# A fp32 two-layer trunk on one NeuronCore: P1 ahead of E0 in the recurrence layer's program

## The chip, the cores and the metric

The kernel runs on one core of a Trainium2 chip. The metric is the device time of one launch in microseconds (us); less is better. Times are medians of several runs, and one run was also taken with the hardware profiler.

## The reference

The input x is (1, 512, 1024) in fp32. Layer 0 mixes the tokens with an RWKV-7 recurrence, layer 1 with a spatial gating unit; a SwiGLU feed-forward network follows each, and RMS norms stand before and behind every part. The change lies in layer 0:

```python
xs = x[None] + xx[None] * mix[:, None, None, :]
r, k, v = jnp.einsum('cbtd,cde->cbte', xs[:3], w_rkv)
decay = jnp.exp(-jnp.exp(w_log)); a = jax.nn.sigmoid(a0 + (xa @ a1) @ a2)
kk = heads(k * k_k); kk = kk / max(norm(kk), 1e-12)
k = k * (1.0 + (a - 1.0) * k_a)
S_t = S_{t-1} diag(w_t) + (S_{t-1} a_t) b_t^T + v_t k_t^T      # 16 heads of 64, 512 steps
y_t = S_t r_t
```

with a_t = -kk and b_t = kk times a. The kernel computes the recurrence in chunks of 64 tokens: cumulative decays, products of pairs within a chunk, the inverse of a triangular matrix per chunk and head, and then a scan over the 8 chunks.

## The kernel before, in words

The 16 heads are worked in four batches b of 256 features, each two feature tiles q of 128. `rwkv()` (L669) walks through the words of the string `PLAN` (L35). The word's letter names a stage and its digit the batch:

```python
for n in PLAN:
    f, b = n[0], int(n[1])
    if f == "P":
        if xr is None:
            xr = mixed_split(0, "ssssssss")
        kr[b] = kr_proj(b)
    elif f == "E":
        ops[b] = early(b, *kr[b])
```

- **P**, `kr_proj` (L807): the projections to k and r. Four units (k for q 0 and 1, then r), each 24 matmuls of 128x512 (tile `proj`), since every fp32 product is made of three: whi with both halves of the activations (`xsp`) and wlo with the upper half. `weight()` (L184) loads a unit's weights by SP's queue into `wraw`, ScalarE casts them to `whi` (L181) and VectorE subtracts to make `wlo` (L182). There are two buffers each of wraw, whi and wlo, so a unit's cast waits for the matmuls of the unit two before it. ScalarE copies the result out of PSUM (L813).
- **E**, `early(b)` (L893): two small matmuls for decay and a; on ScalarE tanh, exponentials (L923, L925) and, for the norm of kk, L936, L940, L941, L942, with table loads between different functions; on VectorE the steps L916, L919 (a scan over the tokens), L926, L932, L945 to L951, L954, L961, L962; on TensorE the norm's sums (`ssp`, L938) and the bonus sums (`bps`, L957). SP's queue stores four results to DRAM, two to `sa` (L964) and two to `sb` (L967). Batches 0 and 2 share one set of buffers for the tiles `tw` and `ta`, batches 1 and 3 another (`tws`).
- **V**, `v_proj` (L851): the value projection, two units of 48 matmuls of 128x256 (`v`) per word, eight units in all, called u0 to u7 here; weights by `weight()` as above, results copied out (`vev`, L867) and stored (`Vd`, L868).
- **F**, `front(b)` (L977): loads `ST` from sb (L982) and `MV` from sa (L988, 16 loads), then makes the products of pairs: eight `lm` (L1004) and four `bkt` (L1018) in two PSUM banks that they share. ScalarE empties an lm with three copies (L1007, L1010, L1012) and a bkt with four (L1022, L1023), and GpSimd cuts triangles out of the copies (L972).
- **B**, `back(b)` (L1026): the inverse. VectorE transposes `LA` to `LX` (L1035), goes through 15 dependent steps of a product (`tm`, L1049) and a subtraction (`Dm`, L1051), and transposes twice (`hn` L1054, `Dt` L1055). TensorE then multiplies blocks up: `mvt` (L1062), `Qp` (L1071), `Np` (L1080), `Tp` (L1083), `Q2p` (L1094), `T2p` (L1103), `mp` (L1112), `gh` (L1119), into `bdT`.
- **X** prepares the value projection's activations, **S**, `scan` (L1124), goes through the chunks, and **N**, `finish`, does the group norm and the gate.

The words give the program's order only. Which instruction comes where on each engine is set by a list scheduler (`schedule_with_timeline_sim=True`, L1428), which takes the program's order as priority and interleaves what its own model holds ready. Each engine then works its row of instructions off in that order, and so does SP's queue of DMAs.

Of the kernel before, what the change touches and what calls it, by code (L numbers as in the profile page):

```python
# [31 lines left out]
BANKS_F1 = dict(tr=(1, 2), gu=(4, 0, 7, 6), R=(4, 0), Q=(3, 5), Z=(7, 6), h0=(1, 2, 0, 5), h1=(4, 3, 7, 6))  # L32
SLOTS = 17
E2 = 7
PLAN = "P0 E0 P1 E1 P2 E2 P3 E3 X0 F0 B0 F1 V0 V1 V2 V3 B1 S0 F2 S1 F3 N0 B2 N1 B3 S2 N2 S3 N3".split()  # L35
XV = "xxxessss"
XSLOTS = 13
LAG = 2
# [94 lines left out]
class Trunk:  # L133
# [535 lines left out]
    def rwkv(self, x0):  # L669
# [3 lines left out]
        with ExitStack() as ctx:  # L673
# [574 lines left out]
            xr, kr, ops, Y = None, {}, {}, {}  # L1248
            for n in PLAN:
                f, b = n[0], int(n[1])  # L1250
# [181 lines left out]
```

## Time and profile before

| | us |
|---|---|
| median of 3 runs | 1315.66 (1313.27 to 1319.33) |
| profiled run | 1315.28 |
| its span, first to last instruction | 1313.6 |
| outside the span | 1.7 |
| TensorE busy | 1257.4 |
| mean granted clock of TensorE | 0.984 of full speed |

A row of a timeline gives the start and length in us, the engine, the line, the operation, output<-inputs, how many instructions were joined, and in brackets the idle time before the row with what ended it. Of the span, 81 to 163 us hold the key and receptance projections, 163 to 227 the value projection with front(0) and parts of back(0) and front(1) between its matmuls, and the recurrence layer goes on up to some 480 us; the rest are the two feed-forward networks and the gating unit.

### The profile page before, as it was taken

Reading aid. Unit: us, or ns where it says so; the run is one execution under the profiler, and the core shown is the slowest. Engines: PE = TensorE matmul, PEld = TensorE weight load, DVE = VectorE, ACT = ScalarE, POOL = GpSimd, SP = SyncE. Lnnn points to the kernel's source line nnn. Section 1 sums busy time; section 2 is a strip of 40 time slices with the busy share of each in tenths; the row PEclk is TensorE's granted clock in tenths of the full one; section 3 lists DMA queues with packets and bytes.
Section 4 is the critical chain, followed back from the end, with each engine's and each line's share of the span. In section 5 each row is a group of like instructions: output and inputs, shape, how many; then the busy total and the mean of one; then the engine's idle time right before and its main releaser. Section 6 shows DMA issues by size and latency. Waiting matters only on the chain.

```text
span 1313.6 us, 24404 instructions
## 1 busy us (share of the span) xinstructions
PE 1257.4 (96%) x9644; PEld 1091.1 (83%) x9644; DVE 988.1 (75%) x1613; ACT 739.4 (56%) x1303; POOL 151.6 (12%) x300
## 2 busy tenths in 40 slices
PE   5999999989899899999999999999989999999998
PEld 3667799978787698999997878878888999998876
DVE  7976766477866687868779977476679877789985
ACT  7986785686444463445546556543454454556553
POOL 0000284566000002100000000020002000000000
PEclk9999999999979999999999999999989999999999
DMA  5137594322243225244344314343430433444322
GB/s 163 34 95 175 146 224 156 88 72 65 75 127 112 75 80 160 68 126 125 92 154 136 122 49 128 94 135 94 144 97 1 129 98 105 120 125 149 113 65 81
DMA packets 219379, 144.29 MB, mean 110 GB/s; under 512 B 67920, under 2 KB 193408, under 8 KB 219264
## 3 DMA queue, kind: packets, MB, share of 16 engines
q1 hardware_dynamic: 217968, 138.01, 36.4%
q0 software_dynamic: 1296, 4.72, 1.1%
q8 instruction: 76, 1.25, 0.4%
q14 instruction: 39, 0.32, 0.1%
HBM read 128.54 MB, written 14.16 MB: 109 GB/s over the span
## 4 chain that ended last, share of the span: by engine, by line
PE 68%; DVE 7%; ACT 2%; issue 1%; DMA 1%; POOL 0%; DVEq 0%; ACTq 0%
PE acc L206 25%; PE Q L206 10%; PE gu L206 9%; PE R L206 7%; PE Z L206 7%; PE u L206 3%; DVE wlo L182 1%; PE gh L1119 1%; PE mp L1112 1%; PE Yp L1161 1%; PE lm L1004 1%; DVE wsum L405 1%; DVE x L336 1%; PE s L1366 1%; PE ptr L281 0%
## 5 line engine op out<-in xcount | busy, mean ns | idle before, releaser
L182 DVE TENSOR_TENSOR wlo<-wraw,whi 128x1024 fp32r<-128x1024 f32 x83 | 103.1, 1244 | 66.5 <-ACT whi L181 57.7
L206 PE MATMUL Q<-bc,whi 128*128 128x256 f32 x816 | 147.3, 281 | 2.2 <-ACT hn L449 2.2
L206 PE MATMUL acc<-whi,ablk 128*128 128x512 f32 x448 | 141.6, 395 | 2.7 <-DVE acc L623 2.7
L181 ACT CAST whi<-wraw 128x1024 fp32r<-128x1024 f32 x83 | 86.9, 1050 | 101.5 <-PE acc L206 29.2
L206 PEld LDWEIGHTS Q<-bc,whi 128*128 128x128 f32 x816 | 125.5, 189 | 2.8 <-ACT hn L449 2.6
L181 ACT CAST whi<-wsum 128x1024 fp32r<-128x1024 f32 x68 | 71.1, 1051 | 85.0 <-PE Q L206 24.3
L206 PE MATMUL gu<-hT,whi 128*128 128x256 f32 (+1 forms) x448 | 112.0, 342 | 3.3 <-ACT hT L62 1.7
L206 PE MATMUL Q<-bc,wlo 128*128 128x256 f32 x408 | 114.6, 281 | 0.0
L206 PEld LDWEIGHTS acc<-whi,ablk 128*128 128x128 f32 x448 | 84.2, 188 | 23.3 <-ACT hn L621 1.8
L206 PE MATMUL Z<-bc,whi 128*128 128x256 f32 x544 | 99.8, 281 | 0.0
L206 PE MATMUL R<-bc,whi 128*128 128x256 f32 x544 | 98.7, 281 | 0.0
L182 DVE TENSOR_TENSOR wlo<-wsum,whi 128x1024 fp32r<-128x1024 f32 x68 | 82.2, 1221 | 21.5 <-ACT whi L181 20.4
L181 ACT CAST whi<-wq 128x1024 fp32r<-128x1024 f32 x51 | 53.5, 1050 | 72.3 <-PE R L206 22.9
L206 PEld LDWEIGHTS gu<-hT,whi 128*128 128x128 f32 x448 | 78.8, 197 | 13.7 <-ACT hT L62 2.4
L206 PE MATMUL acc<-wlo,ablk 128*128 128x512 f32 x224 | 88.5, 395 | 1.5 <-DVE wlo L182 1.5
L182 DVE TENSOR_TENSOR wlo<-wq,whi 128x1024 fp32r<-128x1024 f32 x51 | 65.3, 1284 | 27.6 <-ACT whi L181 27.4
L206 PEld LDWEIGHTS Z<-bc,whi 128*128 128x128 f32 x544 | 84.1, 189 | 0.0
L206 PEld LDWEIGHTS R<-bc,whi 128*128 128x128 f32 x544 | 83.8, 188 | 0.2
L206 PE MATMUL proj<-xsp,whi 128*128 128x512 f32 x256 | 82.4, 401 | 1.3 <-ACT r L813 1.3
L206 PEld LDWEIGHTS Q<-bc,wlo 128*128 128x128 f32 x408 | 77.2, 189 | 0.0
L206 PE MATMUL Z<-bc,wlo 128*128 128x256 f32 x272 | 76.3, 282 | 0.9 <-DVE wlo L182 0.9
L206 PE MATMUL R<-bc,wlo 128*128 128x256 f32 x272 | 76.6, 282 | 0.0
(377 smaller groups left out, 3191.7 us busy)
## 6 DMA issues: line engine op xcount, KB each, us to landing
wc<-in_ffn_w_down_dram SPq DMA_DIRECT2D x38, 512.0 KB, 3.9
wq<-in_ffn_w_gate_dram SPq DMA_DIRECT2D x68, 256.0 KB
wq<-in_ffn_w_up_dram SPq DMA_DIRECT2D x68, 256.0 KB, 4.7
wraw<-in_rwkv_w_rkv_dram SPq DMA_DIRECT2D x24, 512.0 KB, 5.3
wraw<-in_sgu_w_in_dram SPq DMA_DIRECT2D x16, 512.0 KB, 4.3
wraw<-in_ffn_w_gate_dram SPq DMA_DIRECT2D x10, 512.0 KB
wraw<-in_ffn_w_up_dram SPq DMA_DIRECT2D x10, 512.0 KB, 3.9
x<-in_x_dram SPq DMA_DIRECT2D x8, 512.0 KB, 3.6
```

The lines of the kernel that those rows point to most:

```text
L181: self.nc.scalar.copy(hi, src)
L182: self.nc.vector.tensor_tensor(lo, src, hi.bitcast(F32), op=ALU.subtract)
L206: self.nc.tensor.matmul(out, l, r, start=start, stop=stop, skip_group_check=resumed)
L336: v.scalar_tensor_tensor(xts[tt][:, c], f, y[:, 0:1], xts[tt][:, c], op0=ALU.mult, op1=ALU.add)
L405: v.tensor_tensor(s, x, y, op=ALU.add)
L1004: mm(lm[:, cc * P:(cc + 1) * P], st[:, cc].rearrange("p n t -> p (n t)"), mv[:, cc, :, hd, :], start=True, stop=True)
L1112: mm(mp[:, cc * P:(cc + 1) * P], bdT[:, q * NC + 4 * hh + cc].rearrange("p h t -> p (h t)"), mt[:, cc, :], start=True, stop=True)
L1119: mm(gh[:, cc * P:(cc + 1) * P], mt[rows, cc, :], bx[rows, 0:2, cc, :], start=True, stop=True)
L1161: mm(yp[yr, yc], MV[hh, q][:, cc, 1, hd, :], su[:, q, hd, :], start=True, stop=True)
L1366: mm(acc[:, tt * P:(tt + 1) * P], vt[tt][:, m * P:(m + 1) * P], wsT[:, m, :], start=True, stop=True)
```

## The change

One line differs. The projections of batch 1 come ahead of the early stage of batch 0 in the program; every function is the same.

```diff
-PLAN = "P0 E0 P1 E1 P2 E2 P3 E3 X0 F0 B0 F1 V0 V1 V2 V3 B1 S0 F2 S1 F3 N0 B2 N1 B3 S2 N2 S3 N3".split()
+PLAN = "P0 P1 E0 E1 P2 E2 P3 E3 X0 F0 B0 F1 V0 V1 V2 V3 B1 S0 F2 S1 F3 N0 B2 N1 B3 S2 N2 S3 N3".split()
```

The number of instructions on each engine stays the same. What moves is the scheduler's interleaving. First VectorE in the first two projections, where the wlo belong to P1, L945 to L950 and the first pc, Pp and k to early(0), and L916 and L919 with cum to early(1):

```order
-L182 TENSOR_TENSOR wlo<-wraw,whi 128x1024
-L926 COPY pc<-Pp 128x16
-L182 TENSOR_TENSOR wlo<-wraw,whi 128x1024
+L182 TENSOR_TENSOR wlo<-wraw,whi 128x1024 x2
 L945 SCALAR_TENSOR_TENSOR k<-k,nkk,tw 128x512 x2
 L916 TENSOR_SCALAR tws<-tws 128x1024
+L919 SCALAR_TENSOR_TENSOR cum<-rmask,tws 128x512 x2
+L182 TENSOR_TENSOR wlo<-wraw,whi 128x1024 x3
+L926 COPY pc<-Pp 128x16
 L949 TENSOR_TENSOR tw<-k,Pp 128x1024
-L919 SCALAR_TENSOR_TENSOR cum<-rmask,tws 128x512 x2
+L926 COPY pc<-Pp 128x16
```

early(0)'s L949, from which the rest of that stage hangs, stands three wlo later, and early(1)'s scan stands ahead of it. On TensorE, this is where front(0)'s last lm and bkt stand among the value projection's matmuls now, from the 186th of 384 on:

```order
L1004 MATMUL lm<-MV,ST 128x128 x4
L206 MATMUL v<-whi,xsp 128x256
L206 MATMUL v<-wlo,xsp 128x256
L206 MATMUL v<-whi,xsp 128x256 x2
L206 MATMUL v<-wlo,xsp 128x256
L206 MATMUL v<-whi,xsp 128x256
L1004 MATMUL lm<-MV,ST 128x128 x4
L1018 MATMUL bkt<-ident,ST 128x128 x4
L1004 MATMUL lm<-MV,ST 128x128 x4
L206 MATMUL v<-whi,xsp 128x256 x2
L1004 MATMUL lm<-MV,ST 128x128 x4
```

In before, the last bkt of front(0) and the first mvt of back(0) stand so, with all lm of front(0) at least ten value matmuls earlier:

```order
L1004 MATMUL lm<-MV,ST 128x128 x4
L206 MATMUL v<-wlo,xsp 128x256
L206 MATMUL v<-whi,xsp 128x256 x2
L206 MATMUL v<-wlo,xsp 128x256
L206 MATMUL v<-whi,xsp 128x256 x2
L206 MATMUL v<-wlo,xsp 128x256
L206 MATMUL v<-whi,xsp 128x256 x2
L206 MATMUL v<-wlo,xsp 128x256
L1018 MATMUL bkt<-ident,ST 128x128 x4
```

front(0)'s lm lay between the 67th and the 178th value matmul and lie between the 130th and the 194th now; the first lm of front(1) moved from the 262nd to the 310th, the first mvt from the 192nd to the 227th, and Qp from the 313th to the 330th. Last, VectorE in back(0)'s chain of 15 steps (tm and Dm), where the wlo are those of u6 and u7 of the value projection. Before, from the sixth step on, in its middle and behind it:

```order
L1051 TENSOR_TENSOR Dm<-Dm,tm 128x2x10x6
L182 TENSOR_TENSOR wlo<-wraw,whi 128x1024
L1049 TENSOR_TENSOR tm<-LX,Dm 128x2x63
...
L1051 TENSOR_TENSOR Dm<-Dm,tm 128x2x15
L1054 STREAM_TRANSPOSE hn<-Dm 128x32x32
L1055 STREAM_TRANSPOSE Dt<-Dm 128x32x32
L182 TENSOR_TENSOR wlo<-wraw,whi 128x1024
```

And now, from the twelfth step's product on:

```order
L1049 TENSOR_TENSOR tm<-LX,Dm 128x2x48
L182 TENSOR_TENSOR wlo<-wraw,whi 128x1024
L1051 TENSOR_TENSOR Dm<-Dm,tm 128x2x4x12
L1049 TENSOR_TENSOR tm<-LX,Dm 128x2x39
L1051 TENSOR_TENSOR Dm<-Dm,tm 128x2x3x13
L182 TENSOR_TENSOR wlo<-wraw,whi 128x1024
L1049 TENSOR_TENSOR tm<-LX,Dm 128x2x28
```

Both wlo moved: u6's from behind step 6 into step 12, u7's from behind the two transposes to behind step 13. On ScalarE the whi casts of u4 and u5 stand on both sides of the copies of front(0)'s third bkt now. On SP's queue the 16 MV loads of front(0) come ahead of two wraw loads (u4 and u5) that now stand behind them and behind the store of early(3)'s tws and two Vd. The rows of the late scans are the same work in a slightly different order.

## The prediction

> **What bounds the kernel now.** I read the page first, then the busy time by stretch of the recurrence layer's first 263 us, then TensorE's waits there, then the timelines of the engines at the three places where the new order differs.
>
> ```profile
> PE 1257.4 (96%) x9644; PEld 1091.1 (83%) x9644; DVE 988.1 (75%) x1613; ACT 739.4 (56%) x1303; POOL 151.6 (12%) x300
> ```
>
> TensorE is busy for 96% of the span. An edit that only reorders work can win idle TensorE time back, or make more of it; nothing else moves the end. The second view cuts the part that the change touches (span start, end and length; PE, PEld, DVE, ACT, POOL busy; the granted clock; DMA share; GB/s).
>
> ```profile
> 81.00:163.00 82.00, 81.80 (x419) 61.63 (x420) 57.58 (x68) 58.13 (x78) 6.22 (x13) 1.00 0.62 156
> 163.00:200.00 37.00, 35.64 (x309) 33.63 (x308) 22.47 (x24) 31.84 (x61) 30.65 (x49) 1.00 0.95 220
> 200.00:227.00 27.00, 27.00 (x504) 26.69 (x505) 19.26 (x37) 14.51 (x31) 11.68 (x29) 1.00 0.52 172
> 227.00:263.00 36.00, 34.31 (x449) 31.28 (x438) 16.84 (x47) 21.31 (x52) 18.37 (x44) 0.95 0.30 81
> ```
>
> From 81 to 163 us the key and receptance projections run, just where P1 and E0 change places, and TensorE is busy for 81.80 of 82.00 us. So 0.2 us can be won there, and no more. From 163 to 200 (the value projection with front(0) between its matmuls) 1.36 us are idle, from 200 to 227 nothing. TensorE's waits up to 250 us name the rest (total, times, longest),
>
> ```profile
> PE ptr L281 <- DVE hn L736: 7.5, 1, 7.5
> PE proj L206 <- ACT r L813: 1.3, 1, 1.3
> ```
>
> and, from TensorE's timeline (start, length, then line, operation, tiles, and in brackets the idle time before it):
>
> ```profile
> 174.30 2.02 PE L1004 MATMUL lm<-MV,ST 128*128 128x128 f32 x16 [0.64 <-DMA MV<-sa]
> 180.93 1.13 PE L1004 MATMUL lm<-MV,ST 128*128 128x128 f32 x8 [0.72 <-POOL MV L972]
> ```
>
> The 7.5 us lie at the start, in code that is not touched. The 1.3 us lie ahead of the first instruction that moves (ScalarE's rows are the same up to that copy of r) and stay. What the change can remove are the 0.64 + 0.72 us of lm, which are the 1.36 us above.
>
> **The change part by part.** *The projections and early(0).* TensorE's order is the same, row for row, until two thirds through P1, since the scheduler let P1 run ahead of E0's tail already. What moves is E0's vector work, which now stands behind the weight splits (wlo) of P1's next units.
>
> ```profile
> 87.81 1.22 DVE L949 TENSOR_TENSOR tw<-k,Pp 128x1024 f32<-128x1024 f32 x1
> 92.31 1.22 DVE L182 TENSOR_TENSOR wlo<-wraw,whi 128x1024 fp32r<-128x1024 f32 x1
> L206 PE MATMUL proj<-xsp,wlo 128*128 128x512 f32 x96 | 38.7, 403 | 0.1
> 156.72 1.21 DVE L962 TENSOR_TENSOR kp<-kp,cum 128x1024 f32<-128x1024 f32 x1
> ```
>
> The 96 wlo matmuls of this stretch are 12 units of 8, so a unit takes at most 82/12 = 6.8 us. In before, one wlo (at 92.31) follows L949 where in after three stand ahead of it. The third can only be made when the unit whose buffer it takes has been used, one unit after the first: 93.5 + 6.8 = 100.3 us, so L949 starts about 101.5, 14 us later. On VectorE this is free (57.58 busy of 82). Nothing on TensorE waits for it until front(0) reads the result back at the stretch's end, except the bonus matmuls (bps), which the new order puts 50 matmuls later, which at up to 6.8/24 = 0.28 us each is 14 us again. So I cost the delay in this stretch at 0, between -0.2 (all its idle time) and what one bps would wait if those 50 matmuls took a fifth less than the bound, 14 - 11.4 = 2.6 us.
>
> *front(0)'s loads.* early(2) shares tiles with early(0) and inherits most of its delay: at most 14 us. The rows are a scan of early(3), which VectorE's new order has ahead of early(2)'s L962 and the old behind it; SP's queue; two value matmuls that stand 18 apart; and the page's row for the weight loads (its last number is us from issue to landing).
>
> ```profile
> 162.27 2.33 DVE L919 TENSOR_TENSOR_SCAN cum<-rmask,tws 128x512 f32<-128x512 bf16 x2
> 161.35 1.27 SPq L967 DMA_DIRECT2D sb<-kp  x2
> 162.67 5.21 SPq L188 DMA_DIRECT2D wraw<-in_rwkv_w_rkv_dram  x2
> 167.92 13.74 SPq L988 DMA_DIRECT2D MV<-sa  x16
> 212.53 0.28 PE L206 MATMUL v<-wlo,xsp 128*128 128x256 f32 x1
> 214.68 0.28 PE L206 MATMUL v<-wlo,xsp 128*128 128x256 f32 x1
> wraw<-in_rwkv_w_rkv_dram SPq DMA_DIRECT2D x24, 512.0 KB, 5.3
> ```
>
> The scan ends at 164.6 now, so L962 comes out at least 7 us late. I take 12 of 7 to 14: it ends at 157.9 + 12 = 170. In after, the 16 MV loads stand right behind sb<-kp, and two wraw loads (5.21 us) behind them. So they start at 170 + 0.4 instead of 167.92, and the first lm could run 174.30 - 167.92 = 6.4 us later, at 176.8. The new order has TensorE come to it 63 value matmuls later: 174.30 - 0.64 + 63 x 0.119 = 181.2, where 0.119 is (214.68 - 212.53) / 18. The slack is 4.4 us, and both lm waits go: **-1.4 us**. The moved wraw loads are issued at 170.4 + 13.74 + 2.4 (a tws store and two Vd) = 186.5 and land by 192, at 5.3 us; the cast that needs them comes at 198 (below), so nothing waits.
>
> *The clump of lm.* front(0)'s eight lm, now spread over 111 value matmuls, must fit into 64, and the last come in the row lm, bkt, lm, two v, lm. They share two PSUM banks, which ScalarE empties.
>
> ```profile
> L1007 ACT COPY MV<-lm 64x512 f32<-64x512 f32 x16 | 9.3, 580 | 8.2 <-PE lm L1004 8.1
> L1010 ACT COPY LA<-lm 64x256 f32<-64x256 f32 x16 | 5.9, 367 | 0.4
> L1012 ACT COPY BX<-lm 64x256 f32<-64x256 f32 x16 | 5.9, 367 | 0.3 <-PE v L206 0.3
> L1022 ACT COPY BX<-bkt 64x256 f32<-64x256 f32 x16 | 5.9, 366 | 1.1 <-PE bkt L1018 1.0
> L181 ACT CAST whi<-wraw 128x1024 fp32r<-128x1024 f32 x7 | 7.4, 1051 | 0.0
> 197.32 1.05 PE L1004 MATMUL lm<-MV,ST 128*128 128x128 f32 x8
> 198.46 0.58 ACT L1007 COPY MV<-lm 64x512 f32<-64x512 f32 x1 [1.20 <-PE lm L1004]
> ```
>
> An lm's copies cost 0.58 + 0.37 + 0.37 = 1.3 us and begin 198.46 - 197.32 = 1.1 us after its start; four copies of a bkt cost 4 x 0.37 = 1.5, a whi cast 1.05. Call t the sixth lm's start. Its bank is free at t + 2.4; TensorE, after that lm (0.9, since one takes 1.05 to 1.13 and two 2.02) and a bkt (half of that, four matmuls for eight), wants it at t + 1.35: 1.1 us of wait. Then ScalarE has, in its new order, a whi cast ahead of the bkt's four copies, so the bkt's bank is free at t + 2.4 + 1.05 + 1.5 = t + 4.95; TensorE, after the seventh lm and two value matmuls, wants it at t + 3.55: 1.4 us. Together **+2.5 us**. The bounds: 0, if the cast moves behind in time, and 3.5, if the second cast that follows the bkt's copies counts too.
>
> *The inverse's VectorE chain.* back(0)'s 15 dependent steps run on VectorE, and two wlo of the value weights lie between them. In before, one comes after step 6 and one after both transposes; in after, they come after the products of step 12 and after step 13.
>
> ```profile
> 201.09 0.41 POOL L972 TENSOR_SCALAR_AFFINE_SELECT LA<-LA 64x256 f32<-64x256 f32 x1
> 204.21 2.06 DVE L1035 STREAM_TRANSPOSE LX<-LA 128x1024 f32<-128x1024 f32 x1
> 210.36 1.22 DVE L182 TENSOR_TENSOR wlo<-wraw,whi 128x1024 fp32r<-128x1024 f32 x1
> 215.44 0.35 DVE L1049 TENSOR_TENSOR tm<-LX,Dm 128x96 f32<-128x96 f32 x1
> 217.61 2.23 DVE L1054 STREAM_TRANSPOSE hn<-Dm 128x1024 f32<-128x1024 f32 x1
> 200.32 0.60 PE L1062 MATMUL mvt<-ident,MV 128*128 128x128 f32 x4
> 216.73 0.28 PE L206 MATMUL v<-wlo,xsp 128*128 128x256 f32 x1
> 220.57 1.29 PE L1071 MATMUL Qp<-hn,LA 32*32 32x32 f32 x128
> ```
>
> The mvt at 200.32 is after 192 value matmuls. After the 194th in the new order, all of front(0)'s lm are done, so that lm starts at 200.32 + 0.24 - 1.4 + 2.5 - 0.9 = 200.8. LX needs its LA, which was selected 201.50 - 197.32 = 4.2 us after the last lm's start: LX starts at 205.0, against 204.21. From LX to the end of step 12's product are 215.79 - 204.21 - 1.14 (the wlo between) = 10.4 us, so the wlo is done at 205.0 + 10.4 + 1.2 = 216.6. TensorE uses the first wlo of that unit at 216.73 now; in after at 216.73 - 1.4 + 2.5 - 3.1 (front(1)'s three lm and a bkt, which now come later) = 214.7. It waits 1.9 us: **+1.9**, between 1.1 (LX as now, at 204.21) and 2.9 (LX one us later still). The second wlo adds 1.14 to the transpose's start: 217.61 + 0.8 + 1.14 = 219.6, done at 221.8, ahead of Qp, which comes at 220.57 + 3.0 = 223.6. Nothing there.
>
> *Behind it.* bdT of batch 0, which Qp starts, sets the rest; six value matmuls less lie between Np and T2p (0 to 0.7 us more; I take 0). The late scans are reshuffled in a few rows with the same work and I take 0, between -3 and +3, the size of the idle time that the stretches 163 to 200 and 227 to 263 hold together (1.36 + 1.69).
>
> The sum is -1.4 + 2.5 + 1.9 = +3.0 us on the profiled run's own 1315.28: 1318.3. The median of 3 (1315.66) stands 0.4 us above that run, so 1318.7. That is +0.2%; this kernel's measurement can tell about 0.5% (6.6 us) from no change.
>
> **The rivals.**
>
> ```profile
> 228.00:232.00 4.00, 2.54 (x62) 2.51 (x63) 1.47 (x3) 1.75 (x4) 0.00 (x0) 0.91 0.01 4
> 232.00:236.00 4.00, 4.00 (x79) 3.87 (x78) 0.00 (x0) 0.72 (x2) 2.40 (x6) 0.66 0.00 0
> 364.00:376.00 12.00, 11.09 (x199) 10.04 (x198) 5.96 (x9) 7.22 (x15) 0.41 (x2) 0.50 0.13 23
> 440.00:444.00 4.00, 2.48 (x13) 1.77 (x13) 3.48 (x12) 3.10 (x11) 0.00 (x0) 1.00 0.13 42
> ```
>
> *No stall.* ScalarE and VectorE come in time at both places and only the lm waits go: 1315.66 - 1.4 = 1314.3. For it: the scheduler's plan shows where it expects room. Against: the bank times above leave none.
>
> *The clock falls.* After 1.46 us without matmuls in four (228 to 232) the next four were granted 0.66, which costs 4 x 0.34 = 1.4 us; after 1.52 idle (440 to 444) the clock stayed at 1.00. The clump's 2.5 us and the wlo's 1.9 could each set it off: 1318.7 + 1.4 to 2.8, so 1321.5 at the upper end, and 6 us more if it holds as in 364 to 376 (12 x 0.50): 1327.5. The Trainium skill, "TensorE: Matmul & The Clock Gate", Part 1, has the gate fall only after an idle window of about 3.4 us; by that none of these waits would lower it, and the time would stay at 1318.7. The row of 232 to 236 speaks against that rule as it stands, the row of 440 for it.
>
> *Loads too late (slower).* If early(2) ends later than 170 + 4.4 = 174.4 us, the first lm stands at the head of TensorE's queue with the value matmuls behind it, and each us more is a us lost. To lose 6.6 us beyond no change, L962 must end at 174.4 + 6.6 - 3.0 = 178.0 or later, 20 us behind now against 14 for early(0); at 180 the time is 1318.7 + 5.6 = 1324.3. For it: ScalarE's exponentials and their table loads are queued the same way. Against: VectorE has a third of its time free there.
>
> *Faster.* The stretch from 364 at clock 0.50 follows a chain of waits in the late scans; if the reshuffle closes those waits, 12 x 0.50 = 6 us come back with the 1.4: 1308.3. The rows there are nearly the same, which speaks against it.
>
> *Nothing happens.* As TensorE already ran P1 ahead, the order may change too little to matter: 1315.7.
>
> **How the numbers follow.** Forecast 0.48, no stall 0.14, nothing 0.06, clock 0.15 (a third of it beyond 6.6 us), loads late 0.10, faster 0.07. Slower: 0.05 + 0.10 and 0.05 of the forecast's own tail (downstream +3 with the upper bounds) = 0.20; faster 0.07; same 0.73. The range leaves out most of the faster case and the top of the late loads: 1310.5 to 1326.
>
> **What would show it.** Right: no lm wait on MV loads, two waits of lm on ScalarE's copies of 1 to 1.5 us shortly before 201 us, and a v wait on a wlo near 215. Wrong: an lm that waits for a DMA (late loads), a granted clock under 0.9 between 196 and 225, no new wait there, or a changed stretch behind 263 us that moves the end by more than 3 us.

## The result, and the profile after

The changed kernel takes 1330.66 us in the median (1328.59 to 1331.73, 4 runs), the kernel before 1317.49 us (1313.27 to 1319.46, 4 runs). The ratio is 1.010, with a 95% interval from 1.0079 to 1.0122. The forecast was 1318.7 us, no change, with 1326 as its upper end: it was wrong. The profiled run of the changed kernel took 1328.59 us, its span is 1326.9, 13.3 longer than before, and the mean granted clock is 0.981.

The first line of the page has the same 9644 matmuls, busy for 6.8 us more than before (1257.4); the other half of the 13.3 us is idle TensorE.

```profile
PE 1264.2 (95%) x9644; PEld 1096.8 (83%) x9644; DVE 986.8 (74%) x1613; ACT 739.6 (56%) x1303; POOL 147.1 (11%) x300
```

Where the time goes is read from how late the same events come in the two timelines (start in us):

| event on TensorE | before | after | later by |
|---|---|---|---|
| first proj | 49.9 | 48.5 | -1.4 |
| first value matmul | 162.7 | 160.1 | -2.6 |
| last value matmul | 239.9 | 245.5 | +5.6 |
| first gu of the first feed-forward network | 458.2 | 467.1 | +8.9 |
| first Q of the second feed-forward network (FFN1) | 1024.9 | 1032.2 | +7.3 |
| first acc of FFN1 | 1191.2 | 1204.3 | +13.1 |
| end of the span | 1313.6 | 1326.9 | +13.3 |

Two steps stand out, and a smaller one between them: 8.2 us over the value projection (-2.6 to +5.6), some 3 in the scans behind it, and 5.8 in FFN1, 850 us later, in code that no line of the change touches. Now the rows that answer to those of before. The busy time by stretch (start, end and length; PE, PEld, DVE, ACT, POOL busy; granted clock; DMA share; GB/s) has more idle TensorE from 163 us on:

```profile
81.00:163.00 82.00, 82.00 (x407) 62.44 (x407) 54.34 (x64) 58.24 (x78) 1.38 (x4) 1.00 0.56 147
163.00:200.00 37.00, 33.07 (x304) 30.70 (x304) 22.81 (x26) 26.94 (x49) 30.08 (x52) 1.00 0.91 214
200.00:227.00 27.00, 24.83 (x318) 23.51 (x316) 19.10 (x37) 14.13 (x30) 11.27 (x27) 1.00 0.69 206
227.00:263.00 36.00, 33.98 (x566) 31.16 (x562) 12.25 (x29) 21.33 (x50) 18.57 (x47) 0.95 0.25 70
```

From 163 to 200 us, 3.93 us are idle (1.36 before), from 200 to 227 2.17 (nothing before). TensorE's waits up to 270 us name them (total, times, longest); the start's waits are left out.

```profile
PE v L206 <- ACT vev L867: 3.1, 2, 2.8
PE Q2p L1094 <- issue: 1.9, 1, 1.9
...
PE lm L1004 <- POOL MV L972: 1.0, 1, 1.0
PE lm L1004 <- issue: 1.0, 1, 1.0
...
PE v L206 <- DVE wlo L182: 0.2, 1, 0.2
```

The largest is one that the prediction does not have: a value matmul waits for vev. TensorE's timeline shows it, and the two waits of front(0)'s lm:

```profile
175.59 0.28 PE L206 MATMUL v<-whi,xsp 128*128 128x256 f32 x1
178.64 0.39 PE L206 MATMUL v<-whi,xsp 128*128 128x256 f32 x1 [2.78 <-ACT vev L867]
...
182.82 1.95 PE L1004 MATMUL lm<-MV,ST 128*128 128x128 f32 x16
...
199.61 1.13 PE L1004 MATMUL lm<-MV,ST 128*128 128x128 f32 x8 [1.02 <-POOL MV L972]
...
202.09 1.13 PE L1004 MATMUL lm<-MV,ST 128*128 128x128 f32 x8 [0.96 <-issue]
...
217.28 0.39 PE L206 MATMUL v<-whi,xsp 128*128 128x256 f32 x1 [0.33 <-ACT vev L867]
217.85 0.39 PE L206 MATMUL v<-wlo,xsp 128*128 128x256 f32 x1 [0.19 <-DVE wlo L182]
```

The row of 175.59 is the 96th value matmul, the end of the first two units. The next one needs a PSUM bank that ScalarE has yet to empty by the copy vev. ScalarE's timeline of the changed kernel shows what that copy stands behind:

```profile
171.59 1.28 ACT L941 ACT_TABLE_LOAD   x1
172.88 1.15 ACT L941 ACTIVATE tws<-tws,tiny 128x1024 f32<-128x1024 f32 x1
173.94 0.39 ACT L181 CAST g2h<-g 128x256 fp32r<-128x256 f32 x1
174.35 1.28 ACT L942 ACT_TABLE_LOAD   x1
175.64 1.06 ACT L942 ACTIVATE tws<-tws 128x1024 f32<-128x1024 f32 x1
...
178.03 1.05 ACT L867 COPY vev<-v 128x512 f32<-128x512 f32 x2
```

It is early(3)'s chain with two table loads, without a gap, and vev starts 2.2 us after TensorE has stopped. Before, the lm at 180.93 (a row of the prediction) stood exactly at this place, between the 96th and the 97th value matmul. Two more lm and a bkt lay shortly ahead of it, so that TensorE came to the change of banks at 180.2, when early(3)'s last exponential had just ended. ScalarE's timeline of before:

```profile
178.65 1.06 ACT L942 ACTIVATE tws<-tws 128x1024 f32<-128x1024 f32 x1
...
180.86 0.58 ACT L867 COPY vev<-v 128x512 f32<-128x512 f32 x1
```

That vev ran while TensorE was at the lm, and the 97th value matmul did not wait. In the new order the first lm comes 34 value matmuls later, TensorE is at the change of banks at 175.9 with that exponential still under way, and nothing covers the time that the bank takes to come free. That the moved lm make this difference is read from the two traces; no run puts an lm back there.

The value projection as a whole, from its first matmul to its last, before and then after:

```profile
162.60:240.10 77.50, 74.45 (x1019) 71.65 (x1018) 44.88 (x65) 53.43 (x105) 46.25 (x88) 0.98 0.64 166
```

```profile
160.00:245.75 85.75, 77.64 (x1051) 73.17 (x1050) 48.35 (x72) 53.90 (x106) 48.61 (x97) 0.98 0.64 164
```

Of the 8.25 us, 5.06 are idle time (8.11 against 3.05). 1.1 are the 32 bps of batch 2, which lay ahead of the first value matmul before (at 156.47) and lie behind it now (at 162.94). In the other 2.1 us the same matmuls were busy for longer at the same mean clock. Some 1.0 of it is one lm that fell into a stretch of lower clock (at 236.29 us in after, 2.08 us long, with a granted clock of 0.67 from 236 to 240; its like in before, at 236.57, took 1.06 at 1.00); what lengthened the rest is not settled.

FFN1 lost its time in the first quarter. Before and after, from its first Q on:

```profile
1025.00:1065.00 40.00, 38.91 (x329) 38.70 (x329) 34.21 (x35) 19.87 (x26) 0.00 (x0) 1.00 0.44 123
1065.00:1105.00 40.00, 40.00 (x338) 39.82 (x337) 30.60 (x33) 19.71 (x26) 0.00 (x0) 1.00 0.41 118
```

```profile
1032.20:1072.20 40.00, 36.40 (x292) 35.90 (x291) 28.49 (x29) 16.79 (x22) 0.00 (x0) 0.96 0.38 104
1072.20:1112.20 40.00, 38.94 (x327) 38.56 (x326) 31.30 (x34) 19.64 (x26) 0.00 (x0) 1.00 0.40 113
```

3.6 us more are idle in the two windows together, and 40 x 0.04 = 1.6 are clock. The idle time is this wait of TensorE, and VectorE's timeline, of after and then of before, has what is queued ahead of the wlo:

```profile
1056.42 0.39 PE L206 MATMUL Z<-bc,wlo 128*128 128x256 f32 x1 [2.87 <-DVE wlo L182]
```

```profile
1051.14 2.36 DVE L405 TENSOR_TENSOR wsum<-wq 128x1024 f32<-128x1024 f32 x2 [3.06 <-DMA wq<-in_ffn_w_up_dram]
1053.42 0.68 DVE L462 TENSOR_TENSOR cc<-Z,hn 128x512 f32<-128x512 f32 x1
1054.02 1.22 DVE L182 TENSOR_TENSOR wlo<-wq,whi 128x1024 fp32r<-128x1024 f32 x1
1055.15 1.22 DVE L182 TENSOR_TENSOR wlo<-wsum,whi 128x1024 fp32r<-128x1024 f32 x1
```

```profile
1041.39 2.36 DVE L405 TENSOR_TENSOR wsum<-wq 128x1024 f32<-128x1024 f32 x2 [0.69 <-DMA wq<-in_ffn_w_up_dram]
```

In after, the sums of two weight tiles (wsum, L405) stand at VectorE's head and wait 3.06 us for a load, with the wlo that TensorE needs behind them; in before, the same instruction waits 0.69 and no matmul waits for a wlo. The scheduler wrote a new order here, on TensorE, VectorE and ScalarE, though the program's lines are the same. A list of its kind carries on its own simulated time, and a few us of shift in layer 0 are enough for another choice there. That last sentence is an inference; that the orders differ is read from the two programs.

### The profile page after: what moved, and what is told of

Its sections match the earlier page's. It is cut to its first block, busy times and chain, and to the rows that moved or that the text cites. A ratio compares the mean times of both kernels' runs of the same rounds, so it can differ in the third digit from the quotient of the medians.

```text
span 1326.9 us, 24383 instructions
## 1 busy us (share of the span) xinstructions
PE 1264.2 (95%) x9644; PEld 1096.8 (83%) x9644; DVE 986.8 (74%) x1613; ACT 739.6 (56%) x1303; POOL 147.1 (11%) x300
## 4 chain that ended last, share of the span: by engine, by line
PE 68%; DVE 7%; ACT 1%; issue 1%; DMA 1%; SPq 0%; POOL 0%; DVEq 0%; ACTq 0%
PE acc L206 25%; PE Q L206 9%; PE gu L206 9%; PE R L206 7%; PE Z L206 7%; PE u L206 3%; PE gh L1119 1%; DVE wlo L182 1%; PE lm L1004 1%; PE Yp L1161 1%; DVE wsum L405 1%; DMA wq<-in_ffn_w_up_dram 1%; PE mp L1112 1%; DVE x L336 1%; PE s L1366 1%
```

## The experiments

The theory after the result: (a) FFN1's new order costs some 6 us, by itself and wherever layer 0 stands; (b) the rest comes from the value projection, by the vev wait, the lm waits and the place of the two wlo. The rivals: FFN1 lost time because it was reached later, or by the clock, and not by its order; the scans' or the first network's new orders carry the loss; or the vev wait is worth nothing, because another comes in its place.

All kernels compute the same. To hold an order against the scheduler, most of them carry the same addition: edges between neighbours of a row on one engine that set the order of issue and add no semaphore.

```diff
+def pin(tc):
+    by = {i.name: i for i in tc.nc.cur_bb.bb.instructions}
+    for row in PINS:
...
+        for a, b in zip(names, names[1:]):
+            tc.add_manual_dep(by[b], a, mybir.DependencyInfo(mybir.DependencyClass.NoSync, mybir.DependencyReason.DATA), reason="order")
...
+        pin(tc)
```

`PINS` lists the instructions of each engine; below, only the rows that it moves are shown. The time of each is compared with runs of the kernel before on the same chip.

**FFN1 alone, both ways.** `ffn1_old_order` is the changed kernel with FFN1's rows of TensorE, VectorE and ScalarE in the order of before; `ffn1_new_order` is the kernel before with FFN1 in the order of after. On VectorE, around the instruction that waited, the first takes away these rows, which the second puts in:

```diff
-L455 SCALAR_TENSOR_TENSOR cc<-Q,hn 128x512
-L405 TENSOR_TENSOR wsum<-wsum,wq 128x1024
-L182 TENSOR_TENSOR wlo<-wsum,whi 128x1024
-L405 TENSOR_TENSOR wsum<-wq 128x1024 x2
-L462 TENSOR_TENSOR cc<-Z,hn 128x512
-L182 TENSOR_TENSOR wlo<-wq,whi 128x1024
-L182 TENSOR_TENSOR wlo<-wsum,whi 128x1024
```

> The changed kernel, with the instructions of the second feed-forward network alone held in the order that they have in the kernel before (TensorE, VectorE and ScalarE); everything ahead of it stays in the changed order. Theory of two places: the second network lost 5.9 us by its own new order, so 1330.7 - 5.9 = 1324.8, and the offset to before stays at +7 to +8 us from the first network on. Rival of one place: the second network only suffers from starting 7 us later (loads and clock meet it in another phase), so 1330.7 as the changed kernel.

> The kernel before, with the second feed-forward network alone held in the order that it has in the changed kernel. Theory of two places: 1317.5 + 5.9 = 1323.4, with a wait of some 2.9 us of a Z matmul on a wlo near 1050. Rival of one place: 1317.5.

Measured: ffn1_old_order 1324.39 us (1323.04 to 1325.92), 1.0053 of before (1.0036 to 1.0070), so 6.3 us under the changed kernel's median. ffn1_new_order 1324.10 us (1320.67 to 1327.50), 1.0052 (1.0034 to 1.0070), 6.9 us over the kernel before. FFN1's first quarter, in ffn1_old_order and then in ffn1_new_order:

```profile
1035.00:1075.00 40.00, 38.94 (x329) 38.70 (x328) 34.03 (x35) 19.87 (x26) 0.00 (x0) 1.00 0.44 121
```

```profile
1025.80:1065.80 40.00, 36.24 (x291) 35.83 (x291) 28.52 (x29) 16.81 (x22) 0.00 (x0) 0.96 0.39 107
```

The order takes its loss along wherever it goes: 329 matmuls at clock 1.00 in the old one, 291 at 0.96 in the new one, whichever layer 0 runs ahead of it. That settles (a), and the rival that FFN1 was only reached later falls. Half of the change's loss has nothing to do with the stretch that the change touches. Part of the 6 to 7 us is a lower clock that comes with the order (0.96 in this quarter); how much is worked out below.

**Which engine's order it is.** `ffn1_vector_old` puts only VectorE's rows of FFN1 back, `ffn1_tensor_old` only TensorE's. The first, in one of its pieces:

```diff
 L182 TENSOR_TENSOR wlo<-wsum,whi 128x1024 x2
 L426 TENSOR_TENSOR act<-sg,R 128x256
-L405 TENSOR_TENSOR wsum<-wq 128x1024 x2
 L405 TENSOR_TENSOR wsum<-wsum,wq 128x1024
 L182 TENSOR_TENSOR bc<-tsum,bc 128x1024
```

The second, at the start of the pieces that differ (the norm's transposes among FFN1's first products, gu):

```diff
 L206 MATMUL gu<-hT,wlo 128x256
+L206 MATMUL gu<-hT,whi 128x256 x2
+L206 MATMUL gu<-hT,wlo 128x256
+L206 MATMUL gu<-hT,whi 128x256 x2
+L281 MATMUL ptr<-ident,x 128x128 x4
...
-L281 MATMUL ptr<-ident,x 128x128 x4
```

> The changed kernel in its own order, but for VectorE in the second feed-forward network, which goes back to the order of before; TensorE, ScalarE and SP's queue keep the changed order there. Theory that VectorE alone makes that network's loss (its pair of weight sums wsum<-wq, which wait for a weight load, stand ahead of the wlo that TensorE waits for): the 2.9 us wait of Z on wlo goes, and the time is 1330.7 - 5 = 1325.5, as with all three engines put back (1324.4). Rival that TensorE's own new order makes it: 1330.7.

> The changed kernel in its own order, but for TensorE in the second feed-forward network, which goes back to the order of before; VectorE, ScalarE and SP's queue keep the changed order there. Theory that TensorE's order makes that network's loss: its stretch takes 226 us as in before and not 232, and the time is 1330.7 - 5.8 = 1324.9. Rival that ScalarE's order makes it (two copies of Z ahead of the cast that frees a weight buffer, so that the next weight loads start late): 232 us and 1330.7, and since VectorE alone did nothing, no single engine would bring it back.

Measured: ffn1_vector_old 1332.84 us, 1.0108 (1.0083 to 1.0132), and ffn1_tensor_old 1335.41 us, 1.0132 (1.0101 to 1.0164). Neither wins anything back; TensorE's waits in FFN1, of ffn1_vector_old and then of ffn1_tensor_old, are longer than after's 2.9:

```profile
PE Z L206 <- DVE wlo L182: 3.5, 1, 3.5
```

```profile
PE Z L206 <- DVE bc L182: 4.2, 1, 4.2
PE Z L206 <- ACT hn L443: 1.3, 1, 1.3
```

So my reading that VectorE's place of L405 alone makes the wait falls. With the rows of one engine from the other order, some wait of TensorE was as long or longer, so neither VectorE's nor TensorE's rows alone bring the time back, and all three engines' together do. ScalarE's rows alone were not put back, so the rival of the second expectation, that two copies of Z on ScalarE make the next weight loads late, is untested. Which wait starts the chain stays open; the load that VectorE waited for is where the trace shows it, and no run took that load's lateness away by itself.

**The early part alone, and the stretches between.** `early_new_only` is the changed kernel up to the first scan, with the order of before from there on. `scans_new_order` and `ffn0_new_order` are the kernel before with only the late scans, or only the first network's start, in the order of after. For the scans, on VectorE at their start (and the like on the other engines):

```diff
-L1121 TENSOR_TENSOR MV<-gh,BX 128x4x64
-L1122 TENSOR_TENSOR MV<-gh,MV 128x4x64
 L1051 TENSOR_TENSOR Dm<-Dm,tm 128x2x4x12
 L1121 TENSOR_TENSOR MV<-gh,BX 128x4x64
 L1122 TENSOR_TENSOR MV<-gh,MV 128x4x64
 L1049 TENSOR_TENSOR tm<-LX,Dm 128x2x39
+L1121 TENSOR_TENSOR MV<-gh,BX 128x4x64
+L1122 TENSOR_TENSOR MV<-gh,MV 128x4x64
```

For the first network's start, on ScalarE:

```diff
-L62 ACTIVATE hT<-ptr,vecT_97 128x128 x8
+L62 ACTIVATE hT<-ptr,vecT_97 128x128 x4
 L268 ACTIVATE rr<-ss,rc 128x1 x2
-L251 ACTIVATE hn,ss<-x 128x512 x4
-L268 ACTIVATE rr<-ss,rc 128x1 x2
+L251 ACTIVATE hn,ss<-x 128x512
+L62 ACTIVATE hT<-ptr,vecT_97 128x128 x4
```

For early_new_only the first of these two pieces stands the other way round, with + and - exchanged, and the second isn't needed.

> The changed kernel up to the first scan, with the late scans held in the order of before; from there on every engine's order is that of before. Theory of two places: the value projection's stretch alone costs 7.0 us (the offset between the traces goes from -1.4 to +5.65 us there), so 1317.5 + 7.0 = 1324.5. Rival of one place: 1330.7, since all of the loss would follow from the early part.

> The kernel before, with the late scans alone in the order of the changed kernel. From the traces the offset grows there from 5.65 to 8.8 us, so by theory 1317.2 + 3 = 1320. Rival that this growth is only the clock meeting another phase: 1317.2.

> The kernel before, with the start of the first feed-forward network alone in the order of the changed kernel. In the three traces that have the changed order there the offset falls by 1.1 to 1.6 us over the first network, in two that have the old order by 0.2 and 0.4: by theory 1317.2 - 1.2 = 1316, the one place where the new order is better, and a version ahead of both kernels if it is real. Rival: noise of the runs, 1317.2.

Measured: early_new_only 1320.98 us (1317.97 to 1324.23, 7 runs), 1.0022 (0.9998 to 1.0047); scans_new_order 1318.07 us (10 runs), 1.0010 (0.9997 to 1.0022); ffn0_new_order 1316.31 us (12 runs), 0.9989 (0.9973 to 1.0005). The scans' and the first network's orders can't be told from no change, so the 3 us that the table has between the value projection and the first network are no loss that their order makes by itself. The early part costs 3.8 us in early_new_only, whose interval still touches no change, and 7.2 in ffn1_old_order (its 1324.39 against 1317.17), which has the same early rows and the new ones of the scans and the first network; 4 to 7 us is what the medians say. The traces agree that the early rows cost something and that the amount varies: from the start of the first value matmul to that of the last, the four profiled runs with the old rows (before, ffn1_new_order, scans_new_order, ffn0_new_order) took 77.2 to 79.6 us, and the five with the new ones and no edit in this stretch (after, early_new_only, ffn1_old_order, ffn1_vector_old, ffn1_tensor_old) 82.3 to 87.9. In early_new_only the scheduler wrote the first network and FFN1 in the order of before by itself, with no edge set there. That fits the inference above: with the scans' rows as before, its choices are too.

**The vev wait.** `vev_ahead` is the changed kernel with the first two vev ahead of early(3)'s second table load on ScalarE:

```diff
 L181 CAST g2h<-g_4200 128x256
+L867 COPY vev<-v 128x512 x2
 L942 ACT_TABLE_LOAD
 L942 ACTIVATE tws<-tws 128x1024
 L915 ACTIVATE tws<-a,halfb 128x512
 L930 ACTIVATE kp<-tws,hka 128x512
-L867 COPY vev<-v 128x512 x2
```

`vev_on_vector` takes them off ScalarE instead:

```diff
-                        a.copy(t, acc[n])
+                        if qt:
+                            a.copy(t, acc[n])
+                        else:
+                            v.tensor_copy(t, acc[n])
```

> The changed kernel in its own order on every engine, but for ScalarE's first two copies of the value projection's banks (vev), which go three instructions ahead, in front of the exponential of early(3) with its table load. Theory that the 2.8 us wait at the 96th value matmul is ScalarE's queue: the wait falls to under 1 us and the end comes 2.2 us earlier, 1328.5. Rival that early(3), 1.2 us later, hands the loss on to the stores and loads behind it on SP's queue: the waits of the last lm grow by as much and the end stays at 1330.7.

> The changed kernel in its own order, with the first two copies of the value projection's banks (vev) moved from ScalarE to VectorE, which sits idle for 3.2 us at that place; early(3) on ScalarE is not delayed by them. Theory that the 2.8 us wait at the 96th value matmul costs its length: the wait falls to about 0.8 us, the value stretch gets 2 us shorter, 1328.7. Rival that the wait is handed on, as when the copies went ahead on ScalarE: 1330.7.

Measured: vev_ahead 1330.45 us (1328.66 to 1330.83), 1.0099 (1.0084 to 1.0114), no gain; vev_on_vector 1328.11 us (1324.85 to 1331.12, 7 runs), 1.0074 (1.0044 to 1.0105), 2.5 us under the changed kernel's median, with an interval that overlaps the changed kernel's (1.0079 to 1.0122). TensorE's waits from 160 to 240 us, of vev_ahead:

```profile
PE bps L957 <- DVE tws L954: 2.1, 2, 1.9
...
PE v L206 <- DVE wlo L182: 1.0, 2, 0.8
...
PE v L206 <- ACT vev L867: 0.3, 1, 0.3
```

The wait for vev is gone and 2.9 us of others stand in its place: early(3)'s activations came later on ScalarE by the copies, hence its bonus products (tws, L954) on VectorE, and TensorE met the bps 1.9 us too early. In vev_on_vector, where ScalarE's chain goes on, the window of the old wait is full, and a smaller wait for the bonus products comes (their lines have moved by three):

```profile
176.00:180.00 4.00, 3.93 (x33) 3.73 (x33) 2.14 (x4) 3.96 (x5) 3.72 (x8) 1.00 0.92 230
```

```profile
PE bps L960 <- DVE tws L957: 0.9, 2, 0.7
```

In after, TensorE is busy for 1.36 of these four us. So the traces show that the wait hangs on ScalarE's queue, that moving the copies ahead on ScalarE hands it on in full, and that taking them off ScalarE hands on a third of it. A gain in time fits the second, but is not clear of the noise: vev_on_vector's profiled run took 1331.12 us, no less than the changed kernel.

**The two wlo.** `wlo_back` puts the wlo of u6 and u7 back behind step 6 and behind the transposes of back(0)'s chain:

```diff
 L1051 TENSOR_TENSOR Dm<-Dm,tm 128x2x10x6
+L182 TENSOR_TENSOR wlo<-wraw,whi 128x1024
...
-L182 TENSOR_TENSOR wlo<-wraw,whi 128x1024
 L1051 TENSOR_TENSOR Dm<-Dm,tm 128x2x4x12
...
-L182 TENSOR_TENSOR wlo<-wraw,whi 128x1024
 L1049 TENSOR_TENSOR tm<-LX,Dm 128x2x28
...
 L1055 STREAM_TRANSPOSE Dt<-Dm 128x32x32
+L182 TENSOR_TENSOR wlo<-wraw,whi 128x1024
```

> The changed kernel in its own order, but the two wlo in the inverse's chain of 15 steps stand again where before has them (behind step 6 and behind both transposes). The prediction's term of 1.9 us for them: 1330.7 - 1.9 = 1328.8, if it was rightly placed. Rival that the wait near there is set by the copies of the value projection's banks and by LX, which starts when GpSimd has cut LA: 1330.7, no change.

Measured: 1325.02 us (1323.11 to 1327.02), 1.0057 (1.0038 to 1.0075), 5.7 us under the changed kernel's median and so more than the 1.9 of the prediction. In its profiled run, though, the stretch from the first value matmul to batch 1's Qp is only 1.0 us shorter than in after (113.2 against 114.2). The sign is right. Most of what the median has beyond that goes with a higher granted clock in these runs (0.983 in the mean against 0.9795), as worked out below.

**Everything mended.** `mended` is the changed kernel with the edits of ffn1_old_order, wlo_back and vev_on_vector together.

> The changed kernel with three mendings: the second feed-forward network in the order of before on all engines, the two wlo of the inverse's chain back where before has them, and the first two vev on VectorE. Theory that these are the places that lose: 1330.7 - 5.9 - 1.9 (wlo, at least) - 2.0 = 1321, still above before (1317.1) by the clump's two waits and the clock. Rival that the new places of lm pay once the waits around them are gone: under 1317.1.

Measured: 1322.23 us (1320.72 to 1324.44, 12 runs), 1.0034 (1.0019 to 1.0050). The kernel before is still faster, so the recurrence layer's new order has given nothing here, even with the waits closed that the runs could close; the rival that it pays then falls. In mended the two lm waits of 1.0 us each still stand (in TensorE's waits from 160 to 240 us), and from the start of the first value matmul to that of the last it takes 81.1 us, where the kernel before takes 77.2. mended differs from ffn1_old_order by the edits of wlo_back and vev_on_vector alone, and is 2.2 us under its median (1324.39), where the two edits one at a time came to 5.7 and 2.5. So their medians don't add up; the next paragraph has the reason. No version was found that beats the kernel before.

**What the clock adds.** Equal programs differ in time by their granted clock: of the 54 runs of the kernel before, the five with a mean clock of 0.976 or less took 1324.7 us in the mean, the ten with 0.986 or more 1314.7. The span times its mean clock is an estimate of the span at full clock (it also counts idle time at a low clock as if that cost something). Means over the runs of each kernel, the kernel before on the three chips that it was measured on:

| kernel | runs | time, us | mean clock | span x clock, us |
|---|---|---|---|---|
| before, three chips | 11, 23, 20 | 1318.0, 1317.4, 1317.6 | 0.9825, 0.9832, 0.9820 | 1293.3, 1293.5, 1292.2 |
| after | 4 | 1330.4 | 0.9795 | 1301.5 |
| ffn1_new_order | 5 | 1323.9 | 0.9806 | 1296.6 |
| ffn1_old_order | 4 | 1324.4 | 0.9812 | 1297.9 |
| early_new_only | 7 | 1321.3 | 0.9830 | 1297.1 |
| wlo_back | 4 | 1325.1 | 0.9830 | 1300.8 |
| vev_on_vector | 7 | 1327.9 | 0.9803 | 1300.1 |
| mended | 12 | 1322.2 | 0.9809 | 1295.3 |

Single runs scatter by 1 to 3 us about the last column. At full clock the change costs 8 to 9 us of its 13, and the rest is a lower clock. FFN1's order costs 3.3 to 3.6 (against before on the same chip, and as ffn1_old_order under after); the early part 3.8 (early_new_only) to 4.6 (ffn1_old_order), closer together than the medians; wlo_back wins 0.7, near the 1.0 of its trace; vev_on_vector 1.4. The three mendings together win 6.2, and one by one 3.6 + 0.7 + 1.4 = 5.7: here they do add up. mended stays some 3 us above the kernel before on its chip (1295.3 against 1292.2), so the 4.7 us that its median (1322.23 against 1317.51) still lacks are for the most part not the clock. Whether a kernel's order sets its mean clock, or chance does in so few runs, these runs don't separate; in FFN1, where each of the seven profiled runs with the new wait shows the drop (last section) and none of the six without it does, it goes with the order.

## Why the prediction was wrong

The step that failed is "*Behind it*", with its "I take 0, between -3 and +3". It looked at the late scans, where the rows had moved a little, and that was right (scans_new_order: 1.0010). It did not follow the orders to the program's end. They differ once more at the start of the first network, are equal for a long way (512 to 969 us in after) and differ again in FFN1, and FFN1's new order cost 5.8 us of the profiled run, 6.3 and 6.9 in the medians of the two kernels that move it alone: some 3.5 by waits, the rest by the clock that fell behind them. The bound of 3 us was taken from idle time in layer 0 and so could not hold it. The prediction's own sign of being wrong, "a changed stretch behind 263 us that moves the end by more than 3 us", is what happened.

The second failure is a term that is missing. The prediction asked what the moved lm would wait for, and not what they had covered at their old places. The lm at 180.93 stood where the value projection changes PSUM banks. Without it TensorE waited 2.78 us for a copy queued behind early(3)'s table loads. What that wait is worth in time is not clear of the noise (vev_on_vector: 2.5 us in the median, 1.4 at full clock).

Point by point, the rest:

- *The projections and early(0), cost 0.* Right: 82.00 of 82 us are busy, and no bps waited.
- *front(0)'s loads.* L962 of batch 2 ended at 169.4 us (170 forecast). The MV loads started at 173.78 and not at 170.4, since a load of ST and the sb stores stood ahead of them, which I had overlooked; these 3.4 us just fitted into the slack of 4.4 (luck, as far as the start of the loads goes), the first lm ran at 182.82 (181.2 forecast) without a wait, and the **-1.4** came. The rival of late loads did not occur.
- *The clump of lm, +2.5.* Two waits, 1.02 and 0.96, together 2.0 us and at the places named. The profile names GpSimd's triangle (MV, L972) for the first and nothing for the second, but ScalarE's timeline bears the forecast's reason out:

```profile
199.14 0.37 ACT L1012 COPY BX<-lm 64x256 f32<-64x256 f32 x1
...
201.63 0.36 ACT L1023 COPY BX<-bkt 64x256 f32<-64x256 f32 x1
```

The first is the last copy of the sixth lm and ends at 199.51, the second the last of the bkt and ends at 201.99, behind the whi cast that the forecast had there; the waiting lm start 0.1 us after them, at 199.61 and 202.09. So the mechanism was right and the size a little too large.

- *The inverse's chain, +1.9.* u6's wlo started at 216.58 and ended at 217.8 (216.6 forecast), because LX came at 206.93 instead of 205.0. TensorE, itself late by the vev wait, came to it later too, and waited only 0.19 us for a wlo; the 0.33 just ahead is a wait for another vev. So the term was over-sized: wlo_back has the cost at 1.0 us in the trace and 0.7 at full clock, and the 5.7 of its median goes mostly with the clock.
- *The clock.* It fell in FFN1 (below), where the prediction did not look. In the value projection it depends on the run; in after's profile it stayed at 1.00 from 196 to 225 us. The Trainium skill, "TensorE: Matmul & The Clock Gate", Part 1, which has the clock fall only after an idle window of about 3.4 us, is contradicted again by FFN1, where the clock fell behind a stop of 2.87 us.

So the named terms came to -1.4 + 2.0 + 0.2 = +0.8 us, against +3.0, and what was not named made the result: 2.8 us of waiting at the bank change, some 6 us in FFN1 with its clock, and a lower clock and longer matmuls elsewhere, which the runs do not assign to a place.

## What to carry to other kernels

Where a scheduler writes the order, an edit in one stage can change the order of another that it never touches: compare the orders of all engines to the last instruction, and give every place that differs a term of its own. Of a matmul that moves, ask what it covered where it stood (a PSUM bank that comes free, a load) as well as what it will wait for. When a wait is closed, look at what the engine that now goes first makes late: the copy moved ahead on ScalarE only handed its wait on, and on another engine it still handed on a third. Where equal programs differ by their granted clock, compare span times clock beside the medians; here edits that seemed to be worth 5.7 and 2.5 us came to 0.7 and 1.4.

## What the runs showed of the hardware

One wait of the same length, at the same instruction, does not always cost the same. Read in windows of half a us, the granted clock in these stretches is 1.00 or 0.50 (a window that holds an edge lies between), so the figure of a longer window says what part of it ran at half clock. In after, TensorE stood still for 2.78 us from 175.9 on; in ffn1_old_order, whose early rows are the same, for 2.77 from about 177.0 on. The four-us windows around it, of after and then of ffn1_old_order (the last three columns are the granted clock, the DMA share and GB/s):

```profile
176.00:180.00 4.00, 1.36 (x11) 1.36 (x12) 1.81 (x2) 3.97 (x6) 3.70 (x8) 1.00 0.85 193
180.00:184.00 4.00, 4.00 (x36) 4.00 (x36) 3.96 (x5) 0.07 (x2) 1.19 (x2) 1.00 1.03 191
```

```profile
176.00:180.00 4.00, 1.23 (x10) 1.03 (x9) 0.76 (x2) 3.96 (x6) 3.72 (x8) 0.89 0.90 231
180.00:184.00 4.00, 4.00 (x19) 4.00 (x20) 3.96 (x5) 1.18 (x2) 2.27 (x4) 0.50 0.89 192
184.00:188.00 4.00, 4.00 (x29) 4.00 (x28) 3.93 (x5) 0.18 (x1) 0.00 (x0) 0.75 1.01 193
```

The first went on at full clock with 36 matmuls in the next four us; the second got 0.50 and 19, and 4 x (0.11 + 0.50 + 0.25) = 3.4 us of full clock were missing, of which 0.3 fell into the wait itself. FFN1's wait of 2.87 us in after fell on the bad side too:

```profile
1056.00:1060.00 4.00, 3.58 (x22) 3.58 (x23) 2.44 (x4) 0.18 (x1) 0.00 (x0) 0.73 0.47 135
1060.00:1064.00 4.00, 4.00 (x31) 4.00 (x31) 0.75 (x2) 0.12 (x1) 0.00 (x0) 0.84 0.00 0
```

That is 1.7 us behind a wait of 2.9. The other profiled runs show the spread. Behind the vev wait of 2.8 us the clock stayed at 1.00 in after, early_new_only and wlo_back; it was at half for 3.4 us in ffn1_tensor_old, and for 6.8 us in ffn1_old_order and ffn1_vector_old. Behind FFN1's wait, 2.6 to 4.2 us long, it fell in all seven runs that have it: for 3.4 us in after, ffn1_new_order, wlo_back and vev_ahead, for 6.8 us in ffn1_vector_old, ffn1_tensor_old and vev_on_vector. Half the clock for 3.4 us loses 1.7 us, for 6.8 us 3.4. So a wait of nearly 3 us had a price between its own length and a little over twice that, and a single profiled run can't say which; times of kernels with such waits move by some us between otherwise equal programs.
